# Three edits to a two-layer hybrid attention and convolution kernel: set-up of constants after the convolution's first unit, modulation matmuls of the feed-forward in groups of two loads, final norm as one product

## The chip, the cores and the metric

One core of a Trainium2 chip runs the whole kernel in one launch. The metric is device time in microseconds (us): the median of three runs is 1810.37 us before the change (1809.29 to 1812.6).

## The reference

All is fp32. There are 512 latent tokens and 256 context tokens of width 1024, and two layers. In each layer, for latent and context tokens with the same weights:

```python
mx = silu(c) @ w_ada[l] + b_ada[l]            # 6 vectors of 1024: shift, scale, gate, twice
hx = modulate(rmsnorm(x, norm1_g), sh1, sc1)  # h * (1 + scale) + shift
# one projection, four groups: A windowed attention with sink, B conv module,
# C differential attention, D 2-D neighbourhood attention with a bias table (na_rpb)
y  = concat(A, B, C, D) @ w_out
x  = x + g1 * y
x  = x + g2 * swiglu(modulate(rmsnorm(x, norm2_g), sh2, sc2), w_gate, w_up, w_down)   # hidden 2816
# after layer 1
out = rmsnorm(x, final_g)
```

The conv module of group B is a gate (`a * sigmoid(gate)`), a depthwise convolution over 31 taps, a layer norm and a silu. Group C weighs two softmax maps with a lambda, made from four small vectors (`diff_lq1` and so on).

## The kernel before

Every large matmul is made of three: weights and activations are split into a high part (`whi`, rounded to fp32r) and a low part (`wlo`, what is left), and `mm3` (lines 174 to 178) multiplies high by high, high by low and low by high. ScalarE makes the high part (line 141), VectorE or GpSimd the low one (line 143). A weight unit is 128 output columns of all 1024 rows: one load of 512 KB into one of three `wraw` buffers, then the split.

**Order.** All operations are written in one Python program; a planner orders each engine's instructions at build time by a simulated timeline, taking at each moment, of what is ready, what stands first in the program. At run time each engine's queue runs strictly in that order, and an instruction at its head that waits holds all behind it. All DMAs are issued by SyncE (SP) from `dma` (line 97), in one such queue. Buffers are taken from pools; a pool released early gives its space to a later one, and an operation on a new tile waits until the last reader of the old tile in that space is done.

**The start of layer 0.** `setup` makes the stationary operand `cstat` from `c` and `c_ctx` (both tokens' vectors, 32 columns wide). The first modulation vectors come from `ada_gen`: a vector half is four loads of 256 rows x 512 columns (512 KB each) and, per load, 8 matmuls into four 32-row strips of one PSUM tile (line 306); then a bias is added (line 311), a transpose follows (line 321), and columns `mcol` are copied out (lines 325, 328), which the normalised input `hT` needs (lines 1038 to 1042, one eighth `kt` of it at a time). `first_units` (line 1048) then multiplies `hT` by the first three weight units of group B, eighth by eighth.

Right behind it in the program stands `setup_late` (line 1052): it loads the rotary table `cst`, the permutation `perm`, the small conv and lambda vectors (`vrow`, `wrow`, `lv`), the sinks, and the bias table, which is put into a zeroed tile `rpz`, written to DRAM (`rpd`) and copied there 16 times with a shift (`rpt`, lines 276 to 278). Its scratch lies in the pool `x`. What is made: columns of conv weights (`wcol`, `vcol`), lambda (`nlam`), the sinks. Then `proj_b` finishes group B's gate and product `hp` for each of two units (u = 0, 1). The matmuls of u = 0 and the gate of u = 1 are the three of `first_units`, so u = 0 loads no weights. The conv taps (line 873) run on VectorE beside the following projections and the attention of group C.

**The feed-forward.** `f` runs over 22 blocks of 128 hidden columns in parts of 4, 2, 4, 4, 4, 4; each makes a gate unit, an up unit, silu and product, and the split of its `w_down` rows; after each part the down products go to the residual. Layer 0 makes the missing modulation vectors meanwhile: `ada_gen` over 5 vectors of two halves, stepped 10 times in the first `f` and twice in each other (`next(adas, None)`). A half takes four steps; each step takes one load of `araw` (one buffer in layer 0, three in layer 1) and, right behind it, its 8 matmuls. Layer 1 makes one vector so.

**The tail.** In the last part of layer 1 each of four token tiles (i = 0 to 3, two halves of 512 columns) gets gate product (line 1291) and sum (1292) on VectorE, the squares' sum on ScalarE (1293), a product with the final weights `fin` on GpSimd, for i = 3 on VectorE (1295), the sum of the halves (1297, 1298), the power -0.5 on GpSimd (line 121), and the scaling by that factor, on VectorE for the first half (1304) and on ScalarE for the second (1302). Then each half is stored.

Of the kernel before, what the change touches and what calls it, by code (L numbers as in the profile page):

```python
# [8 lines left out]
F32 = mybir.dt.float32  # L9
F32R = mybir.dt.float32r  # L10
AF = mybir.ActivationFunctionType
ALU = mybir.AluOpType
# [37 lines left out]
class Hybrid:  # L50
# [130 lines left out]
    def setup(self):  # L181
# [8 lines left out]
        self.lay = [{} for _ in range(DEPTH)]  # L190
        self.half = self.npg = 0
        self.pre = {}
# [32 lines left out]

    def setup_late(self):

        nc, t, tp = self.nc, self.t, self.tp
        self.cs = self.tl(self.cpool, [P, C_END], "cst")
        self.dma(self.cs, t["cst"])  # L230
        self.perm = self.tl(self.cpool, [P, 256], "perm")
        self.dma(self.perm, t["perm"])
        rows = self.tl(tp, [16, P], "vrow")
        nc.vector.memset(rows, 0.0)
# [7 lines left out]
        nc.vector.tensor_copy(v, pt[:, 0:16])  # L242
        wrow = self.tl(tp, [124, P], "wrow")
        self.dma(wrow, t["conv_w"].rearrange("l k o (c p) -> (l k o c) p", p=P))
# [5 lines left out]
        nc.vector.tensor_scalar(hln, v[:, 4:12], 0.5, None, op0=ALU.mult)  # L250
        lv = self.tl(tp, [P, 4, DEPTH, 32], "lv")
        for i, g in enumerate(("diff_lq1", "diff_lq2", "diff_lk1", "diff_lk2")):
            self.dma(lv[:, i].rearrange("p l c -> p (l c)"), self.bcast(t[g].rearrange("l c -> (l c)"), DEPTH * 32))
        pr = self.tl(tp, [P, 2, DEPTH, 32], "lpr")
        nc.vector.tensor_tensor(pr, lv[:, 0:2], lv[:, 2:4], op=ALU.mult)
# [8 lines left out]
        for l in range(DEPTH):  # L264
# [6 lines left out]
            q["sub"], q["nlam"], q["sinkn"] = sub[:, l:l + 1], nlam[:, l:l + 1], sk[:, 4 * l:4 * l + 4]  # L271
        z = self.tl(tp, [120, RPW], "rpz")
        nc.gpsimd.memset(z, 0.0)
# [22 lines left out]
    def ada_half(self, l, vec, h, raws, b4=None):  # L296

        nc, t = self.nc, self.t
        q = self.lay[l]
        ps = self.ps(self.ada_tag)  # L300
        for kk in range(4):
            raw = raws[kk] if raws else self.ada_load(l, vec, h, kk)
            for a in range(2):
                k = 2 * kk + a
                for j in range(4):
                    nc.tensor.matmul(ps[32 * j:32 * j + 32, 0:P], self.cstat[:, k, :],  # L306
                                     raw[:, a * 512 + j * P:a * 512 + (j + 1) * P], start=(k == 0), stop=(k == NK - 1))
            if not raws:
                yield 0.8
        b4 = b4 or self.ada_bias(l, vec, h)  # L310
        nc.vector.tensor_tensor(b4, ps[:, 0:P], b4, op=ALU.add)
        if vec in (2, 5):
            for v in range(2):
                self.dma(self.modg[l, vec // 3, v, h * 512:h * 512 + 512].rearrange("(j c) -> j c", j=4), b4[v::32, :])
            return
        i, s = (0, vec) if vec < 2 else (1, vec - 3)
        if (i, "m") not in q:
            q[i, "m"] = self.tl(self.cpool, [P, 2, 2, 8], "mcol", 3)
        m = q[i, "m"]
        pt = self.ps(self.ada_tag)  # L320
        nc.tensor.transpose(pt[:, 0:P], b4, self.ident)
        for v in range(2):
            src, dst = pt[:, v:P:32], m[:, s, v, 4 * h:4 * h + 4]
            if s == 0:
                nc.vector.tensor_copy(dst, src)
            else:
                g = self.gcol[:, i * 16 + l * 8 + 4 * h:i * 16 + l * 8 + 4 * h + 4]
                nc.vector.scalar_tensor_tensor(dst, src, 1.0, g, op0=ALU.add, op1=ALU.mult)
# [656 lines left out]
    def layer(self, l):  # L985
# [64 lines left out]
        npool.release()  # L1050
        if l == 0:
            self.setup_late()
        if l == 1:
# [18 lines left out]
        for u in range(2):  # L1072
            for _ in self.mix2(self.proj_b(l, H, c1, u), tp if u else iter(()), 3, False):
                pass
        self.burst, self.ada_tag, self.atags = 0, "pt", [("wraw", 3, F32, self.wst)]
        adas = self.ada_gen([(0, 3)] if l == 0 else [])
# [141 lines left out]
        fin = None  # L1218
        self.atags = [("araw", 1 if cx else 3, F32, fp)]
        adas = self.ada_gen([(0, 5), (1, 0), (1, 1), (1, 3), (1, 4)] if cx else [(1, 5)])  # L1220
        f0 = 0
        for part in (4, 2, 4, 4, 4, 4):
# [41 lines left out]
            for pr in order[1:] + order[:1] if cx and last else order if cx else order[1:]:  # L1264
                for i in pr:
# [24 lines left out]
                    for n, c in enumerate(halves):  # L1290
                        nc.vector.tensor_tensor(tmp[:, c], ps[:, c], g2[0][:, c], op=ALU.mult)
                        nc.vector.tensor_tensor(xs[i][:, c], xs[i][:, c], tmp[:, c], op=ALU.add)
                        nc.scalar.activation(junk[:, c], xs[i][:, c], AF.Square, accum_out=ss[:, n:n + 1])
                        eng = nc.vector if i == 3 else nc.gpsimd
                        eng.tensor_tensor(tmp[:, c], xs[i][:, c], fin[:, c], op=ALU.mult)
                    rs = self.small(1, "rs")
# [3 lines left out]
                    for n, c in enumerate(halves):  # L1300
                        if n:
                            nc.scalar.activation(tmp[:, c], tmp[:, c], AF.Copy, scale=rs)
                        else:
                            nc.vector.tensor_scalar(tmp[:, c], tmp[:, c], rs, None, op0=ALU.mult)
                        self.dma(self.out[0, i * P:(i + 1) * P, c], tmp[:, c])
        fp.release()
        if l:
            h2p.release()
# [65 lines left out]
```

## Time and profile before

| what | value |
|---|---|
| median of three runs | 1810.37 us |
| profiled execution, its own time | 1809.8 us |
| its span on the core | 1808.0 us |
| TensorE busy | 1715.8 us (95%), mean granted clock 0.979 |
| VectorE busy | 941.5 us (52%) |
| ScalarE busy | 586.3 us (32%) |
| GpSimd busy | 216.8 us (12%) |
| DMA | 172.79 MB, mean 96 GB/s |

The span runs from the first to the last instruction of the profiled execution. PE is TensorE, DVE VectorE, ACT ScalarE, POOL GpSimd, SP or SPq the DMA queue of SyncE. In a timeline row stand the start (us from the span's start), the duration, engine, line, operation, out<-in, shapes and how many were merged; in brackets the engine's idle time just before and what ended it.

### The profile page before, as it was taken

To read this page: it belongs to the slowest core of one execution; us is meant where nothing else is said; L and a number is where in the kernel's file an instruction comes from. 1 tells how busy PE (TensorE), PEld (TensorE's weight loads), DVE (VectorE), ACT (ScalarE), POOL (GpSimd) and SP (SyncE) were. 2 spreads that over 40 slices of the span, in tenths; PEclk is the share of its full clock that TensorE was granted. 3 is DMA by queue.
4 is the path that set the end of the run, shared out by engine and by line. 5 is a ranking of instruction groups with operands and counts; after the bars stand their busy time and mean duration, and the time that the engine had idled before them with its cause. 6 is when DMAs were issued, how large, how long until landed. Compare 5 with 4: busy or idle time off the path is not lost.

```text
span 1808.0 us, 26990 instructions
## 1 busy us (share of the span) xinstructions
PE 1715.8 (95%) x11236; PEld 1415.6 (78%) x11236; DVE 941.5 (52%) x1546; ACT 586.3 (32%) x1052; POOL 216.8 (12%) x200
## 2 busy tenths in 40 slices
PE   6898999888999999999999999999988999999997
PEld 4786787666898878888888888878766888888886
DVE  5599656664362442332424347976565445444354
ACT  4223553553151112121120224345355332321322
POOL 1101202340000010000100011130342000000002
PEclk8998999898999999999999999999999999999999
DMA  9351102215134344234231221120225173323321
GB/s 322 89 155 36 45 24 78 82 38 201 60 93 143 121 140 130 83 96 131 62 107 43 83 81 59 49 66 25 89 61 175 36 209 93 105 83 92 117 70 47
DMA packets 187977, 172.79 MB, mean 96 GB/s; under 512 B 17878, under 2 KB 150478, under 8 KB 187726
## 3 DMA queue, kind: packets, MB, share of 16 engines
q1 hardware_dynamic: 187854, 171.06, 31.0%
q8 instruction: 88, 1.44, 0.3%
q14 instruction: 35, 0.29, 0.0%
HBM read 166.76 MB, written 4.52 MB: 95 GB/s over the span
## 4 chain that ended last, share of the span: by engine, by line
PE 81%; DVE 9%; DMA 4%; ACT 2%; issue 2%; POOL 1%; SPq 1%; POOLq 0%; ACTq 0%; DVEq 0%
PE ps L176 19%; PE ps L177 19%; PE ps L178 19%; PE pu L176 4%; PE pu L178 4%; PE pu L177 4%; DVE accd L873 3%; PE pt L616 2%; PE sc L625 2%; PE pt L510 2%; PE ada L306 2%; PE pu L616 1%; DVE Pm L656 1%; SPq L97 1%; DMA araw<-in_w_ada 1%
## 5 line engine op out<-in xcount | busy, mean ns | idle before, releaser
L177 PE MATMUL ps<-h,whi 128*128 128x512 f32 (+1 forms) x1104 | 383.5, 348 | 2.5 <-DVE h L143 2.5
L176 PE MATMUL ps<-h,whi 128*128 128x512 f32 (+1 forms) x1104 | 382.5, 349 | 0.9 <-DVE gt L974 0.9
L178 PE MATMUL ps<-h,wlo 128*128 128x512 f32 (+1 forms) x1104 | 382.9, 347 | 0.0
L141 ACT CAST whi<-wraw 128x1024 fp32r<-128x1024 f32 (+1 forms) x132 | 134.5, 1023 | 445.7 <-PE ps L177 246.8
L143 DVE TENSOR_TENSOR wlo<-wraw,whi 128x1024 fp32r<-128x1024 f32 (+1 forms) x116 | 140.1, 1211 | 199.0 <-ACT whi L141 198.0
L177 PEld LDWEIGHTS ps<-h,whi 128*128 128x128 f32 x1104 | 209.0, 189 | 29.8 <-DVE h L143 3.2
L176 PEld LDWEIGHTS ps<-h,whi 128*128 128x128 f32 x1104 | 207.8, 189 | 29.7 <-issue 2.8
L178 PEld LDWEIGHTS ps<-h,wlo 128*128 128x128 f32 x1104 | 208.8, 189 | 27.5 <-issue 2.0
L176 PE MATMUL ps<-wdhi,zh 128*128 128x512 f32 x440 | 171.7, 392 | 0.4 <-ACT ntmp L381 0.4
L177 PE MATMUL ps<-wdlo,zh 128*128 128x512 f32 x440 | 171.0, 390 | 0.0
L178 PE MATMUL ps<-wdhi,zl 128*128 128x512 f32 x440 | 170.5, 391 | 0.0
L176 PE MATMUL pu<-hT,whi 128*128 128x512 f32 (+1 forms) x456 | 163.2, 358 | 4.8 <-DVE hp L587 2.2
L177 PE MATMUL pu<-hT,whi 128*128 128x512 f32 (+1 forms) x456 | 160.7, 353 | 0.0
L178 PE MATMUL pu<-hT,wlo 128*128 128x512 f32 (+1 forms) x456 | 160.5, 352 | 0.0
L974 DVE TENSOR_TENSOR gt<-ps,g 128x1024 f32<-128x1024 f32 x66 | 80.6, 1222 | 142.7 <-PE ps L178 114.3
L141 ACT CAST wdhi<-wraw 128x1024 fp32r<-128x1024 f32 x44 | 46.1, 1052 | 271.3 <-PE ps L178 181.0
L977 POOL TENSOR_TENSOR x<-x,gt 128x1024 f32<-128x1024 f32 x12 | 29.7, 2474 | 729.8 <-DVE gt L974 729.8
L873 DVE SCALAR_TENSOR_TENSOR accd<-hp,wcol,accd 128x783 f32<-128x783 f32 (+1 forms) x116 | 112.8, 972 | 2.8 <-ACT accd L870 1.2
L1241 DVE TENSOR_TENSOR sg<-sg,ps 128x768 f32<-128x768 f32 (+1 forms) x44 | 36.1, 821 | 144.1 <-PE ps L178 116.1
L176 PEld LDWEIGHTS pu<-hT,whi 128*128 128x128 f32 x456 | 86.5, 190 | 21.0 <-issue 2.6
L176 PEld LDWEIGHTS ps<-wdhi,zh 128*128 128x128 f32 x440 | 82.6, 188 | 19.3 <-issue 1.4
L178 PEld LDWEIGHTS pu<-hT,wlo 128*128 128x128 f32 x456 | 86.8, 190 | 12.7 <-issue 1.8
(263 smaller groups left out, 2730.3 us busy)
## 6 DMA issues: line engine op xcount, KB each, us to landing
araw<-in_w_ada SPq DMA_DIRECT2D x60, 512.0 KB
wraw<-in_w_gate SPq DMA_DIRECT2D x44, 512.0 KB
wraw<-in_w_up SPq DMA_DIRECT2D x44, 512.0 KB
wraw<-in_w_down SPq DMA_DIRECT2D x44, 512.0 KB
wraw<-in_w_in SPq DMA_DIRECT2D x40, 512.0 KB
wraw<-in_w_ada SPq DMA_DIRECT2D x20, 512.0 KB
wraw<-in_w_out SPq DMA_DIRECT2D x12, 512.0 KB
whi<-in_w_ada SPq DMA_DIRECT2D x8, 512.0 KB
```

The source lines that it names most:

```text
L141: nc.scalar.copy(hi, src)
L143: eng.tensor_tensor(lo, src, f32(hi), op=ALU.subtract)
L176: mm(out, st[0], mv[0], start=first, stop=False)
L177: mm(out, st[0], mv[1], start=False, stop=False)
L178: mm(out, st[1], mv[0], start=False, stop=last)
L306: nc.tensor.matmul(ps[32 * j:32 * j + 32, 0:P], self.cstat[:, k, :], raw[:, a * 512 + j * P:a * 512 + (j + 1) * P], start=(k == 0), stop=( ...
L510: self.nc.tensor.transpose(pt[:, (i - a) * P:(i - a + 1) * P], blocks[i], self.ident)
L616: self.burst_of([lambda i=i, j=j: nc.tensor.matmul(po[64 * j:64 * j + 64, 0:P], *parts[j][i], start=(i == n - 1), stop=(i == 0)) for i in ...
L625: return [lambda o=o, q=q[a][r], k=k[b][r], i=i: self.nc.tensor.matmul(o, q, k, start=(i == 0), stop=(i == 2)) for i, (a, b) in enumerate( ...
L873: nc.vector.scalar_tensor_tensor(acc[:, 0:w], hp[:, k:k + w], wc, acc[:, 0:w], op0=ALU.mult, op1=ALU.add)
L974: nc.vector.tensor_tensor(tmp, ps, g, op=ALU.mult)
L1241: nc.vector.tensor_tensor(sg, sg, pss[1][:, 0:W], op=ALU.mult)
```

## The change

`setup_late` is called from inside the loop over `proj_b`, after u = 0 of layer 0, in place of right after `first_units`. Its scratch tiles are slices of one tile of the pool `c1` (tag `PT`, four buffers, which the attention uses later) and no longer tiles of the pool `x`. In the feed-forward, `ada_half` takes two loads, gives two steps to the rest, and then makes the 16 matmuls of both; layer 0 gets two `araw` buffers. In the tail, each half is multiplied by its row factor and the final weights in one VectorE operation.

```diff
-    def setup_late(self):
-        nc, t, tp = self.nc, self.t, self.tp
+    def setup_late(self, pool):
+        nc, t = self.nc, self.t
+        scr = self.tl(pool, [P, NT], "PT", 4)
...
-        rows = self.tl(tp, [16, P], "vrow")
+        rows = scr[0:16, 0:P]
...
-        wrow = self.tl(tp, [124, P], "wrow")
+        wrow = scr[0:124, P:2 * P]
...
-        lv = self.tl(tp, [P, 4, DEPTH, 32], "lv")
+        lv = scr[:, 2 * P:4 * P].rearrange("p (a l c) -> p a l c", a=4, l=DEPTH)
...
-        pr = self.tl(tp, [P, 2, DEPTH, 32], "lpr")
+        pr = scr[:, 4 * P:5 * P].rearrange("p (a l c) -> p a l c", a=2, l=DEPTH)
...
-        z = self.tl(tp, [120, RPW], "rpz")
+        z = scr[0:120, 5 * P:5 * P + RPW]
...
         for kk in range(4):
-            raw = raws[kk] if raws else self.ada_load(l, vec, h, kk)
+            if self.lazy and not raws and kk % 2 == 0:
+                two = [self.ada_load(l, vec, h, kk + a) for a in range(2)]
+                yield 0.8
+                yield 0.8
+            raw = raws[kk] if raws else two[kk % 2] if self.lazy else self.ada_load(l, vec, h, kk)
             for a in range(2):
...
-            if not raws:
+            if not raws and not self.lazy:
                 yield 0.8
...
         npool.release()
-        if l == 0:
-            self.setup_late()
...
             for _ in self.mix2(self.proj_b(l, H, c1, u), tp if u else iter(()), 3, False):
                 pass
+            if l + u == 0:
+                self.setup_late(c1)
...
-        self.atags = [("araw", 1 if cx else 3, F32, fp)]
+        self.atags, self.lazy = [("araw", 2 if cx else 3, F32, fp)], 1
...
                         nc.scalar.activation(junk[:, c], xs[i][:, c], AF.Square, accum_out=ss[:, n:n + 1])
-                        eng = nc.vector if i == 3 else nc.gpsimd
-                        eng.tensor_tensor(tmp[:, c], xs[i][:, c], fin[:, c], op=ALU.mult)
...
                     for n, c in enumerate(halves):
-                        if n:
-                            nc.scalar.activation(tmp[:, c], tmp[:, c], AF.Copy, scale=rs)
-                        else:
-                            nc.vector.tensor_scalar(tmp[:, c], tmp[:, c], rs, None, op0=ALU.mult)
+                        nc.vector.scalar_tensor_tensor(tmp[:, c], xs[i][:, c], rs, fin[:, c], op0=ALU.mult, op1=ALU.mult)
                         self.dma(self.out[0, i * P:(i + 1) * P, c], tmp[:, c])
         fp.release()
+        self.lazy = 0
```

## Rows read from the trace of the kernel before

**Rows 1.** The page, first part: busy us, share, instructions of each engine.
```profile
PE 1715.8 (95%) x11236; PEld 1415.6 (78%) x11236; DVE 941.5 (52%) x1546; ACT 586.3 (32%) x1052; POOL 216.8 (12%) x200
```

**Rows 2.** Windows: stretch, length, busy of PE, PEld, DVE, ACT, POOL, clock, DMA.
```profile
54.00:59.00 5.00, 1.89 (x8) 0.90 (x6) 4.69 (x20) 4.17 (x8) 1.01 (x1) 0.97 1.03 287
59.00:72.50 13.50, 13.50 (x69) 11.59 (x69) 3.84 (x11) 2.98 (x5) 5.78 (x5) 0.88 0.13 25
120.00:170.00 50.00, 43.22 (x297) 36.45 (x297) 48.63 (x67) 20.45 (x37) 10.33 (x4) 0.98 0.27 76
...
542.00:633.00 91.00, 91.00 (x613) 73.63 (x613) 30.58 (x31) 14.00 (x16) 2.40 (x1) 1.00 0.43 133
```

**Rows 3.** Timeline of VectorE, 45 to 55 us.
```profile
45.69 0.29 DVE L311 TENSOR_TENSOR adab<-pt,adab 128x128 f32<-128x128 f32 x1 [1.68 <-DMA wrow<-in_conv_w]
53.81 0.29 DVE L255 TENSOR_TENSOR lpr<-lv 128x128 f32<-128x128 f32 x1 [7.83 <-DMA lv<-in_diff_lk]
...
54.84 0.22 DVE L328 SCALAR_TENSOR_TENSOR mcol<-pt,gcol 128x4 f32<-128x4 f32 x2
```

**Rows 4.** Timeline of TensorE, 43 to 60 us.
```profile
43.67 1.95 PE L306 MATMUL pt<-araw,cstat 128*32 128x128 f32 x64
...
49.38 0.27 PE L321 MATMUL pt<-ident,adab 128*128 128x128 f32 x1
...
53.94 0.40 PE L178 MATMUL pu<-hT,wlo 128*128 128x512 f32 x1
...
58.86 0.58 PE L177 MATMUL sc<-hT,whi 128*128 128x256 f32 x1 [1.26 <-DVE hT L1042]
...
59.45 0.63 PE L176 MATMUL sc<-hT,whi 128*128 128x512 f32 x1
```

**Rows 5.** Timeline of SP, 50 to 77 us.
```profile
50.18 0.38 SPq L97 DMA_DIRECT2D rpz<-in_na_rpb  x1
...
55.09 0.77 SPq L97 DMA_DIRECT2D rpd<-rpz  x1
...
60.53 13.53 SPq L97 DMA_DIRECT2D rpt<-rpd  x16
...
75.56 1.30 SPq L97 DMA_DIRECT2D wraw<-in_w_in  x1
```

**Rows 6.** Timelines of VectorE and TensorE, 82 to 85 us.
```profile
82.61 1.23 DVE L143 TENSOR_TENSOR wlo<-wraw,whi 128x1024 fp32r<-128x1024 f32 x1 [2.43 <-ACT whi L141]
...
84.49 0.50 PE L176 MATMUL pu<-hT,whi 128*128 128x512 f32 x1 [2.17 <-DVE hp L587]
```

**Rows 7.** Timeline of TensorE around modulation groups in the feed-forward.
```profile
926.16 0.39 PE L177 MATMUL ps<-h,whi 128*128 128x512 f32 x1
926.48 0.65 PE L306 MATMUL ada<-araw,cstat 128*32 128x128 f32 x16
...
927.39 0.40 PE L176 MATMUL ps<-h,whi 128*128 128x512 f32 x1
...
1471.54 1.08 PE L306 MATMUL ada<-araw,cstat 128*32 128x128 f32 x32
...
1472.89 0.40 PE L177 MATMUL ps<-h,whi 128*128 128x512 f32 x1
```

**Rows 8.** Timelines of the tail: GpSimd, TensorE, VectorE, ScalarE.
```profile
1790.69 2.86 POOL L1295 TENSOR_TENSOR gt<-x,fg 128x512 f32<-128x512 f32 x2 [0.76 <-DVE x L1292]
...
1796.85 0.39 PE L178 MATMUL ps<-wdhi,zl 128*128 128x512 f32 x1
...
1799.14 1.28 DVE L1291 TENSOR_TENSOR gt<-ps,g 128x512 f32<-128x512 f32 x2
...
1803.74 0.49 DVE L1304 TENSOR_SCALAR gt<-gt,rs 128x512 f32<-128x512 f32 x1 [0.66 <-POOL rs L121]
1803.74 0.72 ACT L1302 ACTIVATE gt<-gt,rs 128x512 f32<-128x512 f32 x1 [1.29 <-POOL rs L121]
```

**Rows 9.** Timeline of VectorE: a scalar_tensor_tensor of 512 columns.
```profile
95.93 0.68 DVE L146 SCALAR_TENSOR_TENSOR qk<-rt,qk 128x512 fp32r<-128x512 f32 x1
```

More of the change, by code (lines that the diff above doesn't have):

```diff
@@ L190, in setup @@
         self.lay = [{} for _ in range(DEPTH)]
-        self.half = self.npg = 0
+        self.half = self.npg = self.lazy = 0
         self.pre = {}
```

## The prediction

> **What bounds the kernel now.** Read the page's engine line first: TensorE is busy 95% of the span [rows 1], so time is to be had only where it waits or where its work is dearer than it need be. The windows say where that is [rows 2]: from 542 to 633 us, in the feed-forward, it is busy 91 of 91 us at a granted clock of 1.00, so there only dear work can be saved. From 54 to 59 us it is busy 1.89 of 5 us, and in 59 to 72.5 its clock is granted to 0.88 only. From 120 to 170 us VectorE is busy 48.63 of 50 us and TensorE 43.22: VectorE sets the pace there, and what reaches it earlier ends earlier. Then read the queues around the hole at 54 us [rows 3 to 6], the small matmuls among the large ones [rows 7], and the tail [rows 8].
>
> **Part A, the set-up moved behind the first unit.** VectorE runs its queue in order. At 45.69 us it adds a modulation bias; the product of the lambda vectors behind it waits 7.83 us, until 53.81, for its transfer [rows 3]. Behind that stand the copy of the last modulation columns (54.84) and with it the second half of the input hT. TensorE's transpose for that copy had begun at 49.38 [rows 4], so the copy could start at about 49.7, 5.1 us earlier. TensorE's supply ends at 53.94 + 0.40 = 54.34, steady work resumes at 58.86, and then at 0.63 us per 512 columns against 0.40 before [rows 4]: after the wait it runs at the lower of its two levels (1.2 and 2.4 GHz). The hole is 58.86 - 54.34 = 4.5 us; some 3.3 us at 0.63/0.40 of the price cost 1.2 more. So the most that the part gives at the end of the first units is -5.7 us.
>
> Whether that survives hangs on SP's queue. The moved step issues a table, a permutation, small vectors, conv weights, lambda vectors, sinks, the fill of the bias rows (50.18), its copy to DRAM (55.09), and 16 copies that make the shifted table, which hold SP from 60.53 for 13.53 us [rows 5]. Only then the next projection's weights are issued (75.56). Their low part is made on VectorE at 82.61, ahead of the product that frees TensorE's next target, and TensorE waits 2.17 us and starts at 84.49 [rows 6]. The conv's first unit issues no transfer of its own (its weights are there), so being behind it moves nothing in SP's order. The scratch now lies in space that I take to be given up by the last modulation weights, whose products end at 43.67 + 1.95 = 45.6 [rows 4]; the fill can then be issued about when it is now. If the 16 copies stay where they are, the weights go out at about 74 instead of 75.56, and 1.5 of the 5.7 us remain. If the copies slip behind the weights, nearly all remains. Copies 5 us later put the weights at 80: +5. Between -5.7 and +5 I take -2.5, nearest to the row that exists. VectorE's and TensorE's small set-up operations keep their number and lie beside the first units.
>
> The Trainium skill (DMA: Bandwidth & Descriptors, Latency and other measured facts) has a transfer's fixed cost of about 2 us fall with a lighter load on the memory. From the copy to DRAM to the first shifted copy it took 5.4 us here (55.09 to 60.53 [rows 5]), with the DMA engines' share at 1.03 [rows 2]. At 2 us for it, an estimate by that page, SP would be free 3.4 us earlier and part A would be worth about -5.
>
> **Part B, modulation matmuls in bursts of 16.** One load feeds 8 matmuls, which the trace shows as 16 records (two for each fp32 matmul). In layer 0's feed-forward there are 5 modulation vectors x 2 halves x 4 loads = 40 groups, and each stands alone between other matmuls, as the last of them at 926.48 [rows 7]. The price of one: from the product ahead (926.16) to the second behind (927.39) is 1.23 us; two products of 512 columns at their usual distance of 0.23 us take 0.46, so a group costs 0.77. In a double one the stretch from its start to the second product behind is 1472.89 - 1471.54 = 1.35 us, in a single one 927.39 - 926.48 = 0.91: the second 16 records cost 0.44. So 0.77 - 0.44 = 0.33 us of each group goes into changing to the 32-column shape and back. 40 groups made 20 pairs: 20 x 0.33 = 6.6 us at most.
>
> The pairs must stay together for that. With one buffer, each group now waits for its own load and is put between whatever runs then. The change issues a pair's loads two steps, one pass over f, ahead with two buffers, so in steady state both are there. But in the first pass the generator is stepped 10 times: four pairs come due at once, each pair's loads wait for the pair before, and a half can run as soon as its own load lands. I count 7 of 20 pairs split until that is caught up: 13 x 0.33 = -4.3. Layer 1 has 8 groups, partly joined already (the x32 [rows 7]): -0.3 to -1. I take -5 for both. Bounds: -7.6 (6.6 and 1) and 0 (all split). A gain reversed, a late load at TensorE's queue head, costs what its landing lacks, but the loads go out no later than now; I leave it in the bound of 0. Loads, matmuls and transposes keep their number.
>
> **Part C, the final norm as one product.** Out go eight products with the final weights, six on GpSimd (2.86 us for two, from 1790.69) and two on VectorE, and the scaling by the factor on ScalarE (0.72) and VectorE (0.49) [rows 8]. In come eight scalar_tensor_tensor on VectorE, 0.68 each by the nearest row of that operation and width [rows 9]. The last matmul ends at 1796.85 + 0.39 = 1797.24. VectorE takes up the last token tile only at 1799.14 [rows 8]: it stands behind the scaling of tile 2, whose factor is made by GpSimd behind those products. Without them VectorE has per tile 1.25 + 1.25 (product, sum), 0.3 (small ones) and 1.36 (two of the new ones), 4.2 us, while TensorE takes 24 matmuls at 0.23 = 5.4 us; so it keeps up and starts the last tile at about 1797.6: -1.5. From that start to the last scaled half were 1803.74 + 0.72 - 1799.14 = 5.3 us. After: products and sums 2.5, second square with its read-out 0.8, two small ones 0.35, the power 0.6, two new products 1.36 = 5.6: +0.3; the first half leaves 0.7 us ahead of the second, so SP's two issues no longer follow each other: -0.6. Sum -1.8. Bounds: -2.9 if the first half of the last tile is done under TensorE's second, +0.5 if the start stays at 1799.14 and nothing overlaps.
>
> The Trainium skill (VectorE: DVE Perf Modes, The perf-mode tier table) gives fp32 operations on one tensor twice the rate of those on two, which speaks against this edit: it replaces the first kind (0.49 [rows 8]) by the second (0.68 [rows 9]). By the bare factor, an estimate from that page, a new product would take 0.98, the last pair 0.6 more, and the part would give -1.2.
>
> **Sum.** -2.5 - 5 - 1.8 = -9.3, on the profiled execution's 1809.8 us (span 1808.0, 1.8 around it): 1800.5. The median of the three runs, 1810.37, is 0.6 higher: 1801.
>
> **Rivals.** (1) *The set-up's transfers come too late*: slower. If the planner's place for the scratch is free only when the first units have been read (67 us), the fill goes out at 67, the copy 4.9 and the 16 copies 10.3 us after it as now [rows 5], and SP is free at 91 instead of 74: the weights come 15.5 us later than 75.56. TensorE then starts the unit of 84.49 in time but lacks the next one's weights, and VectorE has no slack from 120 to 170 to make up for it; I count 12 of 15.5 us as lost. +12 - 5 - 1.8 = +5: 1815. It decides from where the 16 copies end later than about 80. For it: SP issues in order and the copies are ahead of the weights already. Against: that space is last read at 45.6 us if it lies where I think. Chance 0.09. (2) *Bursts split, and SP takes part A back*: 0 for B, -1.5, -1.8: 1807. For it: each group now runs when its own load lands. Against: the loads go ahead by a whole pass. Chance 0.14. (3) *A new order costs elsewhere*: an edit anywhere can change the planner's order in the attention stages, where a stretch like 120 to 170 leaves TensorE idle for 6.8 of 50 us [rows 2]. As much again is +6.8 - 9.3 = -2.5: 1808. Against: the program's order there is untouched. Chance 0.12. (4) *Everything comes through*: -5.7 - 7.6 - 2.9 = -16.2: 1794. Chance 0.12. My forecast, 1797 to 1805: 0.53.
>
> **Numbers.** 0.2%, 3.6 us, is about what a measurement of this kernel can tell from no change. Faster takes the forecast, (4), half of (2) and a quarter of (3): 0.75. Slower takes most of (1): 0.08. The same is the rest, 0.17. The range, 1793 to 1809, leaves out (1) and a little at either end.
>
> **What would show it.** A: the hole before 59 us gone, the lambda product behind hT on VectorE, and the first weights after the 16 copies issued before 75.56. B: about 20 groups of x32 where 40 of x16 stood, and the feed-forward shorter by some 4 to 6 us. C: no GpSimd product in the tail, the last tile taken up within 0.5 us of the last matmul, and some 9 us from there to the end of the span in place of 10.8. Wrong would be a new TensorE wait over 3 us between 60 and 100 us, x16 groups that keep their number, or a last tile that still starts 2 us late.

## The result and the profile after

Medians of four runs each: 1810.84 us before and 1792.51 us after (1789.59 to 1796.62), ratio 0.990 with a 95% interval of 0.9878 to 0.9922: 18.3 us faster. A second series (e18 below) gave 1794.35 and 0.991 (0.9895 to 0.9926). The forecast was 1801, 1793 to 1809: right in sign, half the size, and the measured time lies just under the range. The profiled execution of after, 1796.62 us, is the slowest of its four; its span is 1794.8 (1808.0 before).

The page's engine line of after, to set beside [rows 1], and its windows, beside [rows 2]:

```profile
PE 1711.2 (95%) x11236; PEld 1419.8 (79%) x11236; DVE 942.3 (52%) x1548; ACT 583.1 (32%) x1048; POOL 207.7 (12%) x194
```

```profile
54.00:59.00 5.00, 5.00 (x29) 4.33 (x29) 3.74 (x8) 1.16 (x2) 3.07 (x2) 1.00 0.02 6
59.00:72.50 13.50, 13.03 (x69) 10.65 (x68) 6.45 (x14) 3.97 (x8) 4.50 (x5) 1.00 0.11 22
...
120.00:170.00 50.00, 46.65 (x309) 38.10 (x308) 48.23 (x69) 20.46 (x39) 10.14 (x4) 0.97 0.24 67
```

The hole is gone (5.00 of 5 us busy, 1.89 before), the clock behind it is 1.00 (0.88 before), and from 120 to 170 us TensorE is busy 3.4 us more, with VectorE as full as before. TensorE's first score products of group C's attention, before and then after, come 23 us earlier:

```profile
125.79 1.32 PE L625 MATMUL sc<-qk,qk 32*128 32x512 f32 x12
```

```profile
102.41 0.50 PE L630 MATMUL sc<-qk,qk 32*128 32x512 f32 x2
```

VectorE's and SP's timelines of after, beside [rows 3, 5, 6]:

```profile
50.05 0.23 DVE L333 SCALAR_TENSOR_TENSOR mcol<-pt,gcol 128x4 f32<-128x4 f32 x2 [1.53 <-PE pt L326]
...
57.58 0.17 DVE L235 MEMSET PT<- 16x128 f32 x1
65.11 0.29 DVE L256 TENSOR_TENSOR PT<-PT 128x128 f32<-128x128 f32 x1 [7.37 <-DMA PT<-in_diff_lk]
...
75.25 0.68 DVE L592 TENSOR_TENSOR hp<-qk,pu 128x512 f32<-128x512 f32 x1
...
87.58 1.23 DVE L143 TENSOR_TENSOR wlo<-wraw,whi 128x1024 fp32r<-128x1024 f32 x1 [2.88 <-ACT whi L141]
```

```profile
50.62 0.49 SPq L97 DMA_DIRECT2D PT<-in_conv_w  x1
57.77 0.28 SPq L97 DMA_DIRECT2D PT<-in_conv_b  x1
...
65.17 0.35 SPq L97 DMA_DIRECT2D rpd<-PT  x1
66.66 13.93 SPq L97 DMA_DIRECT2D rpt<-rpd  x16
...
81.31 0.40 SPq L97 DMA_DIRECT2D wraw<-in_w_in  x1
```

The copy of the last modulation columns runs at 50.05 and not at 54.84. The lambda product still waits 7.37 us, but behind hT. SP waits 6.6 us, until 57.77, for the zeros that VectorE writes into the scratch at 57.58, behind its work on hT; so the 16 copies leave 6.1 us later than before and the weights 5.75 us later, the bad case of part A. Yet TensorE's only waits there are of 0.43 and 0.53 us, between 87 and 89 us. The product that frees its target (hp, 75.25) now stands ahead of the late weights' low part (87.58). Before it stood behind that low part (82.61 [rows 6]):

```profile
83.75 0.68 DVE L587 TENSOR_TENSOR hp<-qk,pu 128x512 f32<-128x512 f32 x1
```

The copy to DRAM to the first of the 16 took 1.49 us against 5.44 [rows 5], with a DMA share of 0.11 around it against 1.03 [rows 2]. The Trainium skill (DMA: Bandwidth & Descriptors, Latency and other measured facts) has the fixed cost of a transfer fall with a lighter load on the memory. The trace goes that way; but before the change three loads of 512 KB had been issued just ahead of the small copy, and how much of the 5.44 us was their turn is not separated here.

TensorE in the feed-forward, one joined burst, beside [rows 7], and VectorE in the tail, beside [rows 8]:

```profile
529.38 0.39 PE L178 MATMUL ps<-h,wlo 128*128 128x512 f32 x1
529.70 1.08 PE L311 MATMUL ada<-araw,cstat 128*32 128x128 f32 x32
530.71 0.39 PE L176 MATMUL ps<-h,whi 128*128 128x256 f32 x1
```

```profile
1784.12 0.68 DVE L1296 TENSOR_TENSOR gt<-ps,g 128x512 f32<-128x512 f32 x1
...
1785.38 0.68 DVE L1297 TENSOR_TENSOR x<-x,gt 128x512 f32<-128x512 f32 x1
1785.98 1.41 DVE L1304 SCALAR_TENSOR_TENSOR gt<-x,rs,fg 128x512 f32<-128x512 f32 x2
1787.30 0.69 DVE L1297 TENSOR_TENSOR x<-x,gt 128x512 f32<-128x512 f32 x1
...
1789.79 1.41 DVE L1304 SCALAR_TENSOR_TENSOR gt<-x,rs,fg 128x512 f32<-128x512 f32 x2 [0.66 <-POOL rs L121]
```

Layer 0's feed-forward has 17 whole bursts of x32 where 40 of x16 stood; layer 1's five bursts are unchanged. In the tail the last tile is taken up at 1784.12, with the last matmul's end at 1784.08. But the two products of the tile before stand between the two sums of the last one, and from the last matmul to the span's end it is 10.7 us, 10.8 before.

### The profile page after: what moved, and what is told of

It reads as the page before. It is cut to its first block, busy times and chain, and to the rows that moved or that the text cites. A ratio compares the mean times of both kernels' runs of the same rounds, so it can differ in the third digit from the quotient of the medians.

```text
span 1794.8 us, 26985 instructions
## 1 busy us (share of the span) xinstructions
PE 1711.2 (95%) x11236; PEld 1419.8 (79%) x11236; DVE 942.3 (52%) x1548; ACT 583.1 (32%) x1048; POOL 207.7 (12%) x194
## 4 chain that ended last, share of the span: by engine, by line
PE 80%; DVE 10%; DMA 4%; ACT 2%; issue 2%; SPq 2%; POOL 1%; POOLq 0%; DVEq 0%; ACTq 0%
PE ps L176 19%; PE ps L177 19%; PE ps L178 18%; PE pu L176 4%; PE pu L178 4%; PE pu L177 4%; DVE accd L878 3%; PE pt L621 2%; PE sc L630 2%; PE pt L515 2%; SPq L97 2%; PE ada L311 2%; DVE Pm L661 1%; PE pu L621 1%; DMA wraw<-in_w_in 1%
## 5 line engine op out<-in xcount | busy, mean ns | idle before, releaser
L979 DVE TENSOR_TENSOR gt<-ps,g 128x1024 f32<-128x1024 f32 x66 | 80.6, 1223 | 163.4 <-PE ps L178 149.0
```

What stands on the lines that cost most here:

```text
L979: nc.vector.tensor_tensor(tmp, ps, g, op=ALU.mult)
```

## The experiments

Given are the median, its ratio to the kernel before on the same chip, and the ratio's 95% interval; a gain on the kernel before in us is worked out from the ratio, and two other runs are set beside each other by their medians. Edits are to the kernel before unless another is named.

**The three parts alone, and the set-up taken apart (e1 to e4).** e1: part A's lines of the diff; e2: part B's; e3: part C's.

> The kernel before with part A alone (set-up moved, scratch in the space of c1). Theory T1: A has become worth much more than the -2.5 us forecast: the hole before 59 us (about 5 us) and a new order on VectorE, in which the product that frees TensorE's target and the conv taps stand ahead of the late weights' low part (3 to 4 us more): -9 us, 1801 to 1803. Rival T2 (the forecast's own): SP's queue takes the gain back: -1.5 to -3, and the rest of the -18 is in B and C. Rival T3: much of the -18 is a new order in layer 1 that only all three edits together bring: -4 to -6.

> The kernel before with part B alone (bursts of 16). T1: 17 of 20 pairs joined at 0.33 us: -5.5 to -6.5 us, feed-forward of layer 0 shorter by that, x32 groups in the trace. T2: the same, plus whatever A lacks: -10. If bursts were worth nothing: 0.

> The kernel before with part C alone (final norm as one product). T1: the tail is as long as before, since the two products of tile 2 stand between the sums of the last tile on VectorE: 0 (-0.5 to +0.5), 10.7 us from the last matmul to the end of the span against 10.8. Forecast: -1.8.

e4 moves the lambda part alone:

```
-        lv = self.tl(tp, [P, 4, DEPTH, 32], "lv")     (and its loads, product, sum, Exp)
+    def setup_lam(self, pool):                        (the same, scratch in scr of pool c1)
...
+            if l + u == 0:
+                self.setup_lam(c1)
```

> The kernel before with only the lambda part of the set-up (four loads, product, sum, exponential) behind the conv's first unit; all else of the set-up stays in its old place and scratch. The hole before 59 us must go, but VectorE's order keeps the late weights' low part ahead of the product that frees TensorE's target. T1: only a part of A: -3 to -5 us, with a TensorE wait left near 80 us. T2 (the gain is the hole and nothing else): as much as A alone. If SP takes all back: -1.5.

Measured: A 1796.85, 0.9927 (0.9915 to 0.9939); B 1805.13, 0.9968 (0.9957 to 0.9979); C 1809.17, 0.9997 (0.9987 to 1.0007); lambda alone 1812.74, 1.0015 (1.0006 to 1.0025). So A is -13.2, B -5.8, C -0.5, which can't be told from nothing, and their sum, -19.5, is the whole change within its interval. A is more than even T1 had (-9), and e4 is a miss of all three of its sides. In e4 the hole at 55 us went and came back at 85, VectorE's and TensorE's timelines:

```profile
77.64 0.29 DVE L279 TENSOR_TENSOR PT<-PT 128x128 f32<-128x128 f32 x1 [8.25 <-DMA PT<-in_diff_lk]
```

```profile
85.05 0.80 PE L176 MATMUL pu<-hT,whi 128*128 128x512 f32 x1 [8.36 <-DVE hp L593]
```

The lambda loads then stand behind the 16 copies on SP. Moving the waiting product is not enough: its loads must not fall behind something long.

**Which piece of part A it is: the place of the call, or the scratch's space (e5).**

```
+        if l == 0:
+            self.setup_late(c1)        # ahead of the first unit; scratch in c1 as in part A
         for u in range(2):
```

> Part A with the call ahead of the conv's first unit (u = 0) and only the scratch moved to the space of c1. If the place of the call in the program made the gain: nothing is left of it, 1808 to 1813. T1 as refined: the scratch's space makes it. The set-up's transfers can only be issued when the last modulation weights are read, so the planner, in its own timeline, has the lambda product ready only after hT and puts it there: same as A alone, 1796 to 1798.

Measured: 1794.84, 0.9915 (0.9901 to 0.9929), as part A. With the new space, the call's place is worth nothing that can be told; SP issues the set-up's loads in the same order in e5 and in the whole change. That the planner starts them when it takes the space for free is argued, not shown, and the call's move with the old scratch was not run.

**What SP's queue costs (e6, e7: edits to part A).**

```
-        for c in range(16):
+        for c in [*range(16)] * 2:                    # e6
...
+        if l == 0:
+            self.setup_rpt(c1)                        # e7: bias table behind proj_c's first unit
```

> Part A with the 16 copies of the shifted table issued twice (SP held some 27 us in place of 14). If SP's queue decides what comes after the set-up: the next weights come 14 us later, TensorE and VectorE wait for them: +8 to +13 against A alone, 1805 to 1810. If the new order on VectorE has made SP's hold harmless: 0 to +2, 1797 to 1799.

> Part A with the bias table (fill, copy to DRAM, 16 copies) written behind the first projections of group C in the program; the planner puts 4 of the 16 copies ahead of the next weights and 11 behind. If SP still costs something in A: the weights go out 10 us earlier, VectorE's wait of 2.3 us for their high part near 86 us goes: -1 to -3 against A alone, 1794 to 1796. If SP's hold is harmless there: 1796 to 1798.

Measured: e6 1811.16, 1.0004 (0.9993 to 1.0015); e7 1800.58, 0.9935 (0.9919 to 0.9951). SP's and TensorE's timelines of e6:

```profile
64.75 27.15 SPq L97 DMA_DIRECT2D rpt<-rpd  x32
...
92.61 0.39 SPq L97 DMA_DIRECT2D wraw<-in_w_in  x1
```

```profile
96.28 1.08 PE L307 MATMUL pt<-wraw,cstat 128*32 128x128 f32 x16 [11.12 <-DMA wraw<-in_w_ada]
```

Weights at 92 cost 14 us against e1, all of A's gain and a little more than the side of SP's queue had. Not all of it need be the weights: in e6 group C's attention is back in its old place too (first score product at 132.1 us). But e7, with its weights at 70.75, 9 us earlier than in e1 (79.70), is some 4 us slower than e1 by the medians where 1 to 3 faster was expected: a miss. (By the ratios it is 1.4 us slower, and their intervals overlap; that it is slower at all is not shown by the times.) In the planned order of e7 group C's attention starts in its old place (first score product at 118.3 us; 100.9 in e1, 125.8 before). From 45 to 120 us the two lose about the same (1.1 us of TensorE's time in e7, 0.9 in e1), so between 70 and 81 us the weights' issue decides nothing there; a new suspect is the order.

**The order, and the copies' queue (e9 to e11, e13, e14: edits to part A, but e10).**

```
+            self.setup_rpt(self.tp)      # e9: bias table in its old place and scratch; e10: the table alone as in A
-        nc.vector.memset(rows, 0.0)
+        nc.gpsimd.memset(rows, 0.0)      # e11
-            self.dma(self.rpt[:, c, :], self.rpd[:, 39 - c:71 - c])
+            self.nc.gpsimd.dma_start(self.rpt[:, c, :], self.rpd[:, 39 - c:71 - c])   # e13; e14: nc.scalar
```

> Part A, but the bias table (fill, copy to DRAM, 16 copies) keeps its old scratch and its place ahead of the first units; the vectors and the lambda part stand behind the first unit with scratch in c1. In the planned order the copies come before the small vectors again, the lambda product stays behind hT, and group C's attention keeps its old place on TensorE (its first score product is about the 520th group and not the 394th). Theory (part A's 13 us are the hole, about 5.7, and the earlier place of group C's attention): only the hole comes back, 1803 to 1806, and VectorE is again the later one around 125 us. Rival (the new order is a mere companion; the time comes from the hole and from VectorE's queue between 54 and 85 us): 1795 to 1799, as part A alone.

> Only the bias table moves behind the first unit with scratch in c1; the vectors and the lambda part stay. The wait of VectorE for the lambda loads and TensorE's hole at 55 us stay, the 16 copies come later on SP by some 5 us, and group C's attention keeps its old place. Theory (the late copies cost what the late weights lack, and nothing pays for it): slower than before by 2 to 6 us, 1812 to 1816. Rival (late weights are harmless, since the conv's products now run ahead of their low part on VectorE): 1809 to 1811.

> Part A with the zeros of the vector rows written by GpSimd and not by VectorE, whose queue made the small vectors' loads, and behind them the 16 copies and the weights, wait until 57.6 us. The planned order of VectorE is part A's without that one entry. Theory (SP's queue still costs in part A: the weights go out at 80 us, the copies doubled cost 14 us more): the copies leave 5 to 7 us earlier, the weights at about 74, and the time is 2 to 5 us under part A alone: 1792 to 1795. Rival (with VectorE's products of the conv ahead of the weights' low part, the weights have slack, and only a far later issue hurts): no change from part A, 1796 to 1798.

> Part A with the 16 copies of the bias table issued by GpSimd's queue and not by SP's. SP then reaches the weights right behind the copy to DRAM, at about 65 us in place of 79.7. The planned order has group C's attention in its old place (first score product about the 519th group on TensorE, 394th in part A). Theory (of part A's 13 us some 7 are the hole and VectorE's queue behind it and some 5 the earlier place of group C's attention, which fills VectorE's stretch from 120 to 170 us): about -7 to -9 against before, 1801 to 1804, TensorE busy 42 to 43 of 50 us in 120 to 170. Rival (the order is a companion, SP's queue is what costs in e7 and e9): as part A or better, 1793 to 1797.

> Part A with the 16 copies issued by ScalarE's queue. The planned order has group C's attention in part A's early place (396th group). The copies stand ahead of the ReLU of the conv's second unit on ScalarE. If ScalarE's queue is held for them as SP's was, some 13 us from 66 us on, that ReLU is late, TensorE waits for its target and loses up to 10 us: 1800 to 1806, with the wait in 68 to 85 us. If ScalarE issues them in much less time, SP's queue is free, the order is the early one, and the time is below part A alone: 1790 to 1794.

Measured: e9 1806.91, 0.9986 (0.9975 to 0.9996); e10 1812.88, 1.0015 (1.0006 to 1.0025); e11 1801.3, 0.9947 (0.9932 to 0.9961); e13 1800.28, 0.9949 (0.9931 to 0.9967); e14 1806.33, 0.9989 (0.9975 to 1.0004). e10 came as the theory had it, e13 and e14 just outside what it had (TensorE is busy 43.51 of 50 us in e13's stretch from 120 to 170); e9 was slower than both sides had it, and e11 4.5 us slower than part A where it should have been faster: two misses. TensorE's timelines of e9, e11 and e14 show a new hole in each:

```profile
71.08 0.20 PE L241 MATMUL pt<-ident,PT 16*128 16x16 f32 x1 [4.80 <-DMA PT<-in_diff_subln_g]
```

```profile
69.78 0.50 PE L176 MATMUL pu<-hT,whi 128*128 128x512 f32 x1 [3.50 <-ACT qk L582]
```

```profile
80.59 0.79 PE L176 MATMUL pu<-hT,whi 128*128 128x512 f32 x1 [13.75 <-ACT qk L582]
```

In e9 the small vectors now stand behind the copies on SP, and their transpose at TensorE's head waits for them. In e11 GpSimd's queue reached the zeros at 58.78 us, later than VectorE's (57.58 in after); the loads followed, and with them the lambda product. Its Exp stands ahead of the conv's ReLU on ScalarE, whose timeline in e11 and in e1 is:

```profile
67.54 0.20 ACT L259 ACTIVATE ls<-ls 128x4 f32<-128x4 f32 x1 [2.94 <-DVE ls L258]
...
68.59 0.86 ACT L582 ACTIVATE qk<-sc 128x512 f32<-128x512 f32 x2
```

```profile
64.97 0.20 ACT L259 ACTIVATE ls<-ls 128x4 f32<-128x4 f32 x1
...
66.03 0.86 ACT L582 ACTIVATE qk<-sc 128x512 f32<-128x512 f32 x2
```

2.6 us later in the Exp, 2.6 in the ReLU, 3.0 more in TensorE's wait (0.47 in e1). Part A has no slack there. In e14 ScalarE itself is held:

```profile
67.18 12.71 ACTq L280 DMA_DIRECT2D rpt<-rpd  x15
79.94 0.87 ACT L582 ACTIVATE qk<-pu 128x512 f32<-128x512 f32 x2 [12.95 <-DMA rpt<-rpd]
```

With a hole of 13.75 us e14 is still no slower than before.

**Part B: bursts or buffers (e12), and part C's order (e8), A with B (e15).**

```
-        self.atags = [("araw", 1 if cx else 3, F32, fp)]
+        self.atags = [("araw", 2 if cx else 3, F32, fp)]                                   # e12
...
-                            nc.vector.tensor_scalar(tmp[:, c], tmp[:, c], rs, None, op0=ALU.mult)
+                            nc.vector.scalar_tensor_tensor(tmp[:, c], xs[i][:, c], rs, fin[:, c], ...)   # e8: first half alone
```

> The modulation weights of the feed-forward get two buffers, as in part B, but one load and its 8 matmuls per step as before, so the groups of x16 are not joined by the program. Theory (part B's gain is the groups joined to bursts of x32): nearly all groups stay x16, and the time is that of before within 1.5 us: 1809 to 1812. Rival (the gain is the second buffer, loads that are there earlier): 1804 to 1806, as part B alone.

> The kernel before with another tail: the first half of each tile as one product with factor and weights on VectorE; of the second half the product with the weights ahead of the factor (GpSimd, VectorE for the last tile) and the scaling on ScalarE. VectorE has one new product less between the last tile's operations, and the last scaling runs on two engines: -1 to -2 us against before, 1808.5 to 1809.5. If the tail is bound by the chain square, power, scaling, store alone: 0.

> Parts A and B without part C (the final norm as before). Theory (part C moves nothing, parts A and B add up: 13.2 + 5.8): 1790.5 to 1793.5, as the whole change within its uncertainty. Rival (part C takes back some 2 us where VectorE is fuller at the end): 1788 to 1790. Other rival (part C helps once A and B have moved the rest): 1794 to 1796.

Measured: e12 1805.75, 0.9982 (0.9972 to 0.9992); e8 1808.8, 0.9994 (0.9985 to 1.0003); e15 1795.22, 0.9915 (0.9896 to 0.9934). e12 is a miss of the theory: with a second buffer and nothing else the planner joins the groups by itself, 16 whole ones of x32 in layer 0's feed-forward:

```profile
528.76 1.08 PE L306 MATMUL ada<-araw,cstat 128*32 128x128 f32 x32
```

e8 and e15 agree with a part C that moves nothing that these runs can tell. The median of e15 lies in the range of its other rival (part C helps once A and B have moved the rest), but its interval takes in the whole change's 0.990 and 0.991.

**What part B gives back (e16 to e18).** In the profiles with the second buffer (e2, e12, e15, the whole change) TensorE waits 2.75 to 4.67 us at the end of layer 1's attention. VectorE and TensorE in e2, then in e1:

```profile
1368.36 1.23 DVE L143 TENSOR_TENSOR wolo<-wraw,wohi 128x1024 fp32r<-128x1024 f32 x1 [2.38 <-ACT wohi L141]
1370.66 1.22 DVE L143 TENSOR_TENSOR wolo<-wraw,wohi 128x1024 fp32r<-128x1024 f32 x1 [1.07 <-ACT wohi L141]
1371.80 0.68 DVE L528 COPY PT<-pt 128x512 f32<-128x512 f32 x1
```

```profile
1372.54 0.70 PE L620 MATMUL pu<-PT,VA 128*64 128x128 f32 x4 [4.67 <-DVE PT L528]
```

```profile
1360.82 1.23 DVE L143 TENSOR_TENSOR wolo<-wraw,wohi 128x1024 fp32r<-128x1024 f32 x1 [2.51 <-ACT wohi L141]
1361.96 0.68 DVE L525 COPY PT<-pt 128x512 f32<-128x512 f32 x1
```

```profile
1362.70 0.55 PE L617 MATMUL pu<-PT,VA 128*64 128x128 f32 x6 [0.93 <-DVE PT L525]
```

The copy that TensorE wants stands behind one product more, and each of these waits for its own weights. The edit paces those weights differently:

```
-        self.beside(self.chain(self.a_attn(l, 0), self.a_attn(l, 1)), more(), 2 * dn, 12)
+        self.beside(self.chain(self.a_attn(l, 0), self.a_attn(l, 1)), more(), 2 * dn, 8 if l else 12)
```

> The whole change, with the output weights' preparation in layer 1's attention paced at 8 in place of 12 steps. In VectorE's planned order the last copy of turned probabilities then stands behind three low-part products and not five. Theory (the copy held behind products that wait for their weights is what part B gives back there): TensorE's wait of 2.75 us ahead of the output projection falls under 1.2 us, its granted clock around it stays higher, and the time is 2 to 4 us under the whole change measured beside it, 1788 to 1791. Rival (the wait is one of many and the next takes its place): within 1 us of it.

> The kernel before with that pace of 8 alone. There the copy stands behind four products and moves ahead of the fourth. Theory: TensorE's wait for it was 0.87 us and its removal gives at most 1: 1808.5 to 1811. Rival (the pace helps by itself, whatever part B does): 1806 to 1808.

> The whole change again, as the partner of e16 on the same chip: 1790 to 1795, ratio 0.988 to 0.992.

Measured: e16 (the whole change with it) 1786.82, 0.9869 (0.9851 to 0.9887), faster than both kernels; e17 (without the change) 1805.14, 0.997 (0.9958 to 0.9981); e18 (the whole change beside them) 1794.35. VectorE and TensorE in e16:

```profile
1346.86 3.98 DVE L143 TENSOR_TENSOR wolo<-wraw,wohi 128x1024 fp32r<-128x1024 f32 x3 [0.77 <-ACT wohi L141]
1353.54 0.69 DVE L529 COPY PT<-pt 128x512 f32<-128x512 f32 x1 [2.70 <-PE pt L515]
```

```profile
1354.29 1.09 PE L621 MATMUL pu<-PT,VA 128*64 128x128 f32 x14 [0.17 <-DVE PT L529]
```

VectorE now waits for TensorE. The pace gives 7.5 us on the whole change where 2 to 4 were expected, and 4.5 (5.4 by the ratio) without it, where 1 at most was: it helps by itself, as e17's rival had it, by more than the wait that I meant to remove. The 2 to 3 us between the two would be what part B's order had cost, but each of the three ratios is known to no better than 2 to 3 us either way, so these times don't show it.

## Why the prediction was half the size

The table cuts each profiled execution at TensorE's rows: the first score product of group D (sd) in layer 0, the first and last up-projection product (ps<-h) of layer 0's feed-forward, the last sd of layer 1, the first ps<-h of layer 1, the last matmul, the end. "Lost" is TensorE's idle time plus its busy time x (1 - granted clock), summed over windows from 45 to 120 and from 120 to 285 us. A range is that of the kernels of a line.

```
                               to D       to FF      FF l0      to l1 end  l1 attn end  FF l1      tail       lost 45-120  120-285
before,e2,e3,e8,e12,e17   282.1-284.1 214.1-217.1                                                              6.7-9.1   14.7-16.7
whole,e1,e5,e15,e16,e18   274.3-276.2 212.5-213.7                                                              0.9-2.0   12.5-13.4
e7  (weights early)             276.8       215.3                                                                  1.1        16.2
e9  (table old)                 281.9       216.1                                                                  6.3        16.2
e11 (zeros on GpSimd)           280.4       213.7                                                                  7.9        13.4
e13 (copies on GpSimd)          277.5       216.8                                                                  4.0        13.8
e14 (copies on ScalarE)         287.6       211.8                                                                 17.5        11.2
without second buffer                             553.5-554.1 267.1-268.7 101.5-106.5 369.2-371.1  10.3-11.0
with it (5 kernels)                               547.1-547.8 267.1-267.3 108.1-110.7 369.2-370.5  10.7-10.8
paced: e16, e17                                   547.8,553.5 267.2,268.8   99.4,99.0       372.0  10.6,10.7
```

**Part A, -2.5 forecast, -13.2 alone: the step that failed is SP's taking it back.** The bound of the hole, -5.7, was too large, and that it agrees with the loss from 45 to 120 us, which falls by 5.9 (7.6 to 1.7, means of the first two lines), is luck. In smaller windows, 4.1 of these are the hole's own, from 54 to 72.5 us (4.6 to 0.5). I had counted 4.5 us of hole as lost, but in it TensorE was idle for only 3.1 (busy 1.89 of 5 us [rows 2]). Another 1.7 come from 72.5 to 120 us (2.9 to 1.2), where the wait behind hp was. From the bound I took 3.2 for the weights that go out late. The premise, copies late means weights late, was right, and worse than I took (81.31). What failed is its last link: I left VectorE's order as it was, where the wait of 2.17 us [rows 6] came from the weights' low part standing ahead of hp. The change replans that order. e7 shows how little the weights' issue decides up to 81 us, and e6 that 92 is too late (TensorE waits 11.12 us). Then 2.5 us more come between 120 and 285 us (15.6 to 13.1), all of them from 120 to 170 (7.7 to 5.2), and 2.6 from there up to the feed-forward (215.8 to 213.2). I had named the stretch from 120 to 170 us as VectorE's and written that what reaches it earlier ends earlier, and yet put no gain from it into the sum: a term at nothing without a reason. In all kernels of the second line group C's attention begins at 101 to 102 us and not at 124 to 126. Those with the old start and no hole lose 16.2 (e7) or 13.8 us (e13) from 120 to 285, those with the early place in the order and a new hole 13.4 (e11) and 11.2 (e14): the early place goes with the smaller loss, but e13 comes close to it without, and e6 too (13.2, though its stages lie later in the fixed window), so how much is the order's own is not settled. By the feed-forward part A has given 10.6 us in these means; the rest of the 13.2 is spread too thin to be placed.

Rival (1), transfers too late, named the right threat with the wrong point: SP was free at 80.6, past its 80, and from 85 to 120 us only 1.1 us were lost. It did happen where the lambda part moved alone (e4), the table alone (e10), or the copies doubled (e6). In e10 hp, too, stands ahead of the late low part (80.45 and 90.16), but the rotary products that TensorE needs next stand behind it (93.32, where after has them ahead, at 83.43), and TensorE waits 2.9 us. The pieces don't add: e4 is +2.7 and e10 +2.7, vectors and lambda without the table (e9) -2.5, all together -13.2. Rival (4), 1794, came nearest in the number, but by luck: it had -5.7, -7.6 and -2.9 where the parts gave -13.2, -5.8 and nothing.

**Part B, -5 forecast, -5.8 alone: the size right, the account wrong.** The feed-forward is 6.3 us shorter by the means of the kernels with the second buffer and without, near the upper bound of 6.6: 17 pairs whole, not 13, which at the 0.33 us worked out are 5.6 of it. It is work saved and not waits for loads: in that stretch TensorE idles 1.8 us before and in e2, at a granted clock of 1.00 in both. Layer 1's share, -0.3 to -1, is 0. Not forecast was what is given back at the end of layer 1's attention, 300 us behind the feed-forward, 4.8 us by the means of the profiles (109.4 and 104.6). One changed place in VectorE's order is seen there, and TensorE's wait for it is 1.8 to 3.8 us longer than e1's; that it makes all of the 4.8 is argued, and the 2 to 3 us of e16 to e18 are within their noise. That is rival (3), with a place found. That the program must pair the loads was wrong: buffers do it (547.1 in e12). The located terms sum to less than the measured -5.8 and, in e12, -3.3; the means of the profiles don't settle that difference.

**Part C, -1.8 forecast, 0.** The term that failed is the stretch from the last tile's start to its last product. The tile starts 0.04 us behind the last matmul (1.90 before), and 1.9 us are won there where 1.5 were forecast. The 5.6 us from there to the last product's end became 7.1 (1784.12 to 1791.20; 5.3 before), which gives 1.8 back: I had VectorE do the last tile's work in one piece, and the two products of the tile before (1.41 us) are queued in the middle of it. 5.6 + 1.4 = 7.0 is that miss. The first half's store does go out 0.7 us ahead of the second's, as forecast (1790.57 and 1791.23), but the -0.6 for it doesn't show: from the last product's end to the span's end it is 3.6 us, 3.5 before. A new product takes 0.7 us, as the near row said. The 0.98 that I had worked out by the Trainium skill's factor (VectorE: DVE Perf Modes, The perf-mode tier table), put on the whole duration of 0.49, is too much here.

**Of the things named to show it**, the hole gone, the lambda product behind hT, the shorter feed-forward, no GpSimd product and the early last tile came; weights ahead of 75.56 and a tail of 9 us did not. Of the three signs of being wrong none came, though the working was wrong. The last rows of the table show where the paced version's gain lies: 9 us at layer 1's attention end against the whole change, 1.5 of them lost behind.

## What to carry to other kernels

Where a planner lays out the queues, price an edit's effect on the order of each engine and not its instructions alone: pieces of one move gave +2.7, +2.7 and -2.5 us and the whole -13, by what each left ahead of what. A late transfer need not cost: in part A nothing that another engine needed soon stood behind it, in e6 it did. Look there before charging it. A second buffer can join work that no program order joins, and what it moves may surface far behind the edit.

## What the runs showed of the hardware

- Issuing one copy of 120 x 32 elements holds the queue 0.85 us on SP (27.15 for 32) and as long on ScalarE (12.71 for 15), which computes nothing meanwhile. On GpSimd, in e13, 16 of them took 10.5 us:

```profile
67.86 5.42 POOL L280 DMA_DIRECT2D rpt<-rpd  x9
73.83 1.05 POOL L280 DMA_DIRECT2D rpt<-rpd  x2 [0.56 <-issue]
75.77 2.62 POOL L280 DMA_DIRECT2D rpt<-rpd  x5 [0.89 <-issue]
```

- A hole of TensorE costs more than its length. e14's of 13.75 us ended at 80.59, and the window around its end (columns as in [rows 2]) has a granted clock of 0.50, the lower of the two levels, for the 4.41 us of work in it; in e1, busy throughout, it is 1.00:

```profile
72.50:85.00 12.50, 4.41 (x10) 3.47 (x11) 3.76 (x5) 2.73 (x4) 0.00 (x0) 0.50 0.22 50
```

```profile
72.50:85.00 12.50, 12.50 (x77) 10.69 (x75) 11.01 (x13) 0.04 (x1) 0.00 (x0) 1.00 0.36 96
```
